# Four blocks by halves in front of a norm, three behind it, and split weights in the common tile ring

## The chip, the cores and the metric

The kernel runs on one core of a Trainium2 chip. The metric is device time in microseconds (us) of one execution; the median over several runs is compared. The engines are PE (TensorE, the matmuls), PEld (its weight loads), DVE (VectorE), ACT (ScalarE), POOL (GpSimd) and SP (SyncE, which issues most DMA transfers). Each engine works through its own list of instructions in the order that the program fixed, and waits where an operand is not ready or a buffer not free.

## The reference

512 tokens of 1024 features, float32. The part that matters here is the last step of the first block, and the shape of the two layers behind it.

```python
def rms_norm(x, g):
    y = x * lax.rsqrt(jnp.mean(x * x, axis=-1, keepdims=True) + EPS)
    return y * g
# block 1: forgetting attention, S5 scan, memory attention, gated and merged:
#   x = rms_norm(x + merged @ w_out, g_final)
# block 2, for l in 0, 1 (mod, gates: columns of silu(c) @ w_ada[l] + b_ada[l]):
#   h = rms_norm(x, g) * scale + shift;  x += gate * (dilated attentions(h) @ w_out[l])
#   h = rms_norm(x, g) * scale + shift;  x += gate * (relu(h @ w_f1)**2 @ w_f2)
```

(The second half of the code is told in shortened form.) A norm needs the sum of squares over all 1024 features of a token, so over all eight blocks of 128 features that the product in front of it makes, and every product behind it needs the normed tokens.

## The kernel before

**Products.** Activations lie feature-major: a tile holds 128 features of 512 tokens. Each float32 operand is split in two parts, hi and lo, and a product is three matmuls (hi by hi, lo by hi, hi by lo; `mm3`, L108 to L110). A block of 128 output features is 8 x 3 = 24 matmuls of 512 columns.

**Weights.** They come from HBM in 346 pieces of [128, 1024] (some are 768 wide) by SP's queue, into `wr` (3 buffers). `split` makes hi on ACT (`wh`, a cast, L88) and lo on DVE or POOL in turn (`wl`, a subtraction, L90). `wh` and `wl` have pools of their own, three buffers of [128, 1024] each. `get` splits three pieces ahead and fetches three more ahead of these.

**The ring.** Every other tile of 128 x 512 words (activations, logits, temporaries) comes from one ring of NU = 73 tiles. A tile is taken when the oldest with its place in the ring is released.

**In front of a norm.** `tail` makes the last two blocks of the product by halves of the tokens: first tokens 0 to 255 of both blocks, then tokens 256 to 511 of both. `post` adds the residual (DVE, `x`, L961 or L1070), squares it (ACT, `sq`, L174) and adds the squares up (DVE, `sacc`, L175). `tail` is called in eleven places: behind block 1 ("out"), behind the attention of each layer (`out0`, `out1`), and behind each of the four parts c of the MLP's second product (`f2`) in both layers.

**Behind a norm.** `norm` gives three stages for a half of the tokens. `stat`: sums over partitions (PE, `sumcols`, L181), mean (DVE, `nv`, L199), power -1/2 (POOL, `nr`, L201), broadcast (PE, `bcast`, L188). `hi`: x times scale times the broadcast (DVE, `hu`, L551) and `h` (ACT, L215), for eight blocks. `lo`: `l` (DVE, L223). `head` calls `stat(0)`, `hi(0)`, gets the weights, calls `stat(1)` and `lo(0)`, and then makes the first HN = 2 blocks of the next product by halves of the tokens, all products with `h` first (L584, L585) and those with `l` behind (L588). The norm between block 1 and layer 0 has a longer `stat` (L1067 to L1073, L1743 to L1746): two sums, a reciprocal, two powers on POOL and a product.

**The four norms that are followed by a head.** Here they are named by the product behind them: qa0 (block 1 to layer 0), f10 (MLP of layer 0), qa1 (layer 0 to layer 1), f11 (MLP of layer 1).

**Background.** `ada_gen` makes the modulation columns of a layer on DVE (`adacc`, L505, L511; `fin`, L482, on PE) beside other work; `drain` runs what is left of it. `load2` issues the rope and mask loads on ACT's queue.

**Order.** A scheduler lays down each engine's list when the program is built; the code's calls give the order in which work is offered to it.

Of the kernel before, what the change touches and what calls it, by code (L numbers as in the profile page):

```python
# [17 lines left out]
T = 512  # L18
# [9 lines left out]
class Core:  # L28
# [14 lines left out]
    NU = 73  # L43
    NW = 3, 3, 3

    def u(self, dt=F32, name="u"):
        """a [128, 512] tile of four-byte words from the common ring."""
        self.n += 1
        return self.ring.tile([128, T], dt, tag="u", name=f"{name}_{self.n}", bufs=self.NU)

# [28 lines left out]
    def split(self, i):  # L79
# [6 lines left out]
        h = self.t(self.wp, [128, 1024], F32R, "wh", self.NW[1])  # L86
        l = self.t(self.wp, [128, 1024], F32R, "wl", self.NW[2])
        self.nc.scalar.copy(h[:, 0:n], r[:, 0:n])  # L88
        eng = self.nc.gpsimd if i % self.WP == self.WP - 1 else self.nc.vector
        eng.tensor_tensor(out=l[:, 0:n], in0=r[:, 0:n], in1=f32(h)[:, 0:n], op=ALU.subtract)  # L90
        self.hl[i] = (h, l)

    def get(self, name, kb):
        """the next piece: hi and lo as [128, kb, columns]."""
# [7 lines left out]
        n = self.strips[i][1].shape[-1]  # L102
        return tuple(t[:, 0:n].rearrange("p (k c) -> p k c", k=kb) for t in self.hl.pop(i))

# [7 lines left out]
    def fm(self, out, w, c0, act, kb):  # L112
        """feature-major block: out[128 features, tokens] from strip columns c0..c0+128."""
        (wh, wl), (ah, al) = w, act
        for k in range(kb):
            self.mm3(out, wh[:, k, c0:c0 + 128], wl[:, k, c0:c0 + 128], ah[k], al[k], k == 0, k == kb - 1)

    def tm(self, out, ws, act, tok, cols=slice(0, 256)):
        """token-major block: out[128 tokens, cols]; ws: pieces that follow one another along k."""
        ah, al = act  # L120
        mm = self.nc.tensor.matmul
        ks = [(wh[:, k, cols], wl[:, k, cols]) for wh, wl in ws for k in range(wh.shape[1])]
# [31 lines left out]
    @staticmethod  # L154
    def half(t, hf):
        """half of the tokens: of four blocks of 128 in order, two."""
# [20 lines left out]
    def sumcols(self, pq, sacc, cols):  # L177
        """pq[:, i]: sums over features of the tokens of 128-blocks; cols: lists of first columns that add up."""
# [4 lines left out]
    def bcast(self, r):  # L183
        """columns r [128, n] -> [128, n * 128] in PSUM, the same in every row."""
# [7 lines left out]
    def rstd(self, sacc, cols):  # L192
        """broadcast of 1/sqrt(mean + eps), in PSUM."""
# [10 lines left out]
    def hsplit(self, src, bias=None, out=None):  # L204
        """hi, lo of src (+ bias)."""
# [20 lines left out]
class Att(Core):  # L226
    """Softmax attention on split operands. A head's logits come twice: query-major for the row
    maximum, key-major for the weights that multiply V and a block of ones, which sums them."""

    @staticmethod  # L230
    def cut(t, c):
        """columns c of t: a slice, or (i0, i1) for those of the tokens 4 i + r in the order (r, i)."""
# [5 lines left out]
    def byblock(t):  # L238
        """t, tokens 4 i + r in blocks of 128 and within these in the order (r, i), as [p, r, block, i]."""
# [24 lines left out]
    def turn(self, mc, psum_tag):  # L264
        """columns [128 tokens, 4, 128] -> rows [128, 512] in PSUM (exact)."""
# [5 lines left out]
    def rows(self, mc, tag, psum_tag, out=None):  # L271
        """the same as bf16 in SBUF; of these the last 32 if out is given."""
# [9 lines left out]
    def unit(self, nh, sregs, tregs, qk, vsl, dst, extra=None, nq=4, hd=64, orow=None, fold=None):  # L282
        """Items of a unit of nh heads (pairs of heads share 128 rows of output).
        sregs(qb): tiles of regions (c0, n, piece, q slice, k slice, mask)
        tregs(): tiles of (regions, [(v piece, kb, columns)])
        fold(j): the tile whose other half takes the rows of -max (else these come by a product of their own)
        qk(j, piece) -> pairs (q, k); vsl(j, piece, kb) -> (hi, lo); dst(j) -> (tile AP rows, row0)"""
# [118 lines left out]
        def vrow(j):  # L406
            """rows of a head's values in its sum; the other half holds the sum of the weights."""
# [41 lines left out]
    def mix(a, b, z=1.0):  # L449
        """a and b as one list, spread evenly, b over the first part z."""  # L450
# [3 lines left out]
    def merge(self, a, b):  # L454
        """run items of a with those of b spread evenly among them."""
# [13 lines left out]
class Blk2(Att):  # L469
    def ada_gen(self, l):  # L470
        """columns [128, 48] of silu(c) @ w_ada[l] + b_ada[l]."""
# [6 lines left out]
        def fin(acc, c):  # L478
            """acc: rows of two parts, c and c + 1"""
# [36 lines left out]
    def load2(self):  # L516
        """constants of the second block"""
# [21 lines left out]
    def norm(self, x, gcols, shcols, h):  # L539
        """by half of the tokens: hi and lo of rms(x) * g + shift. Returns the stages stat, hi, lo."""  # L540
# [21 lines left out]
    def plain(self, x):  # L562
        return lambda h, mod, ada: self.norm(x, mod[:, 0:8], ada[:, 0:8], h)
# [126 lines left out]
    HN = 2  # L690
# [1341 lines left out]
```

## Time and profile before

| | |
|---|---|
| median of 3 runs | 2513.65 us (2512.61 to 2514.68) |
| profiled execution, span | 2516.8 us |
| PE busy | 2388.2 us (95%), 12162 matmul instructions |
| DVE, ACT, POOL busy | 1533.0 (61%), 1038.1 (41%), 812.3 us (32%) |
| mean granted TensorE clock | 0.969 of full |

The profiled execution's only time on record is its span; it is 3.1 us over the median of the runs. PE is the busiest engine, and is idle in 129 us; what it loses besides lies in stretches at a lower granted clock, which the 40 slices of the page show as 8 or 7 where a full slice shows 9.

### The profile page before, as it was taken

What the parts mean: (1) busy time and instruction counts of PE and PEld (TensorE: products, weight loads), DVE (VectorE), ACT (ScalarE), POOL (GpSimd) and SP (SyncE); (2) the same over time, 40 slices, a digit from 0 to 9 for tenths busy, and PEclk for the clock granted to TensorE, in tenths of its full rate; (3) what the DMA queues carried; (4) which work ended last, traced back from release to release, by engine and by line L of the source; (5) the groups of instructions that cost most, each with busy time, mean ns of one, the idle gap of its engine ahead of it and who ended that gap; (6) DMA issues with size and microseconds to landing.
All of it is one profiled execution on the core that took longest, in us unless ns stands there. A gap on an engine that the chain in (4) does not pass through costs nothing. (4 is left out here: it accounts for less than half of the span.)

```text
span 2516.8 us, 32068 instructions
## 1 busy us (share of the span) xinstructions
PE 2388.2 (95%) x12162; PEld 1978.9 (79%) x12162; DVE 1533.0 (61%) x2394; ACT 1038.1 (41%) x1639; POOL 812.3 (32%) x601
## 2 busy tenths in 40 slices
PE   7999989989998889999999999998999999999999
PEld 6876778767888777787787888886777777888888
DVE  7667766666998887555459663258864726522222
ACT  4445543452333447533333423433663423423432
POOL 2445354634221552142122121227311612222121
PEclk9999999999998999998899999999999979999999
DMA  5311113213674321121138553233111313222232
GB/s 183 98 47 55 57 61 108 94 59 135 237 264 172 113 76 51 51 85 66 50 102 301 176 209 101 93 114 99 59 51 50 93 34 117 84 94 99 93 101 84
DMA packets 105610, 265.28 MB, mean 105 GB/s; under 512 B 13664, under 2 KB 23408, under 8 KB 105456
## 3 DMA queue, kind: packets, MB, share of 16 engines
q1 hardware_dynamic: 104304, 261.47, 31.2%
q8 instruction: 96, 1.57, 0.3%
q10 hardware_dynamic: 1152, 1.77, 0.2%
q14 instruction: 58, 0.48, 0.1%
HBM read 244.69 MB, written 9.44 MB: 101 GB/s over the span
## 5 line engine op out<-in xcount | busy, mean ns | idle before, releaser
L108 PE MATMUL pmm<-h,wh 128*128 128x512 f32 (+1 forms) x2232 | 855.7, 385 | 14.7 <-ACT h L213 3.9
L110 PE MATMUL pmm<-h,wl 128*128 128x512 f32 (+1 forms) x2232 | 852.9, 382 | 3.7 <-POOL wl L90 2.8
L109 PE MATMUL pmm<-l,wh 128*128 128x512 f32 (+1 forms) x2232 | 853.4, 383 | 0.0
L90 POOL TENSOR_TENSOR wl<-wr,wh 128x1024 fp32r<-128x1024 f32 (+1 forms) x173 | 422.5, 2442 | 1315.4 <-ACT wh L88 1094.4
L88 ACT CAST wh<-wr 128x1024 fp32r<-128x1024 f32 (+1 forms) x346 | 358.2, 1036 | 928.5 <-PE pmm L109 726.4
L108 PEld LDWEIGHTS pmm<-h,wh 128*128 128x128 f32 x2232 | 424.5, 190 | 96.7 <-ACT h L213 4.8
L110 PEld LDWEIGHTS pmm<-h,wl 128*128 128x128 f32 x2232 | 424.5, 190 | 82.5 <-POOL wl L90 3.8
L109 PEld LDWEIGHTS pmm<-l,wh 128*128 128x128 f32 x2232 | 425.2, 191 | 76.5 <-DVE l L221 0.7
L90 DVE TENSOR_TENSOR wl<-wr,wh 128x1024 fp32r<-128x1024 f32 (+1 forms) x173 | 225.1, 1301 | 168.9 <-ACT wh L88 166.5
L383 DVE TENSOR_TENSOR pl<-pe,ph 128x512 fp32r<-128x512 f32 (+4 forms) x168 | 121.7, 733 | 139.7 <-ACT ph L381 138.9
L961 DVE SCALAR_TENSOR_TENSOR x<-pmm,ada,x 128x512 f32<-128x512 f32 (+1 forms) x100 | 64.2, 643 | 213.9 <-PE pmm L110 213.7
L311 PE MATMUL ps<-qk,qk 128*128 128x512 f32 (+4 forms) x416 | 147.9, 386 | 16.1 <-POOL qk L672 9.6
L505 DVE SCALAR_TENSOR_TENSOR adacc<-adw,cact,adacc 128x512 f32<-128x512 f32 x168 | 154.3, 928 | 3.2 <-DMA adw<-in_wada 0.3
L221 DVE TENSOR_TENSOR l<-r,h 128x512 fp32r<-128x512 f32 x64 | 59.3, 928 | 121.6 <-ACT h L213 121.3
L379 ACT ACTIVATE pe<-ps 128x512 f32<-128x512 f32 (+4 forms) x168 | 84.5, 503 | 80.8 <-PE ps L311 72.7
L311 PEld LDWEIGHTS ps<-qk,qk 128*128 128x128 f32 x416 | 83.1, 204 | 37.7 <-POOL qk L672 11.5
L108 PE MATMUL pmm<-yh,wh 128*128 128x512 f32 (+1 forms) x244 | 94.1, 389 | 3.9 <-ACT yh L1403 2.4
L110 PE MATMUL pmm<-yh,wl 128*128 128x512 f32 (+1 forms) x244 | 93.7, 386 | 0.0
L109 PE MATMUL pmm<-yl,wh 128*128 128x512 f32 (+1 forms) x244 | 93.0, 382 | 0.0
L381 ACT CAST ph<-pe 128x512 fp32r<-128x512 f32 (+4 forms) x168 | 88.8, 528 | 9.4 <-DVE pl L383 3.5
L402 PE MATMUL ppv<-pl,v 128*128 128x512 f32 (+2 forms) x216 | 79.0, 366 | 4.1 <-DVE pl L383 4.0
L400 PE MATMUL ppv<-ph,v 128*128 128x512 f32 (+2 forms) x216 | 79.0, 366 | 2.7 <-ACT ph L381 1.6
(365 smaller groups left out, 3863.2 us busy)
## 6 DMA issues: line engine op xcount, KB each, us to landing
wr<-in_w SPq DMA_DIRECT2D x324, 512.0 KB
adw<-in_wada SPq DMA_DIRECT2D x192, 256.0 KB
xs<-xg SPq DMA_DIRECT2D x136, 64.0 KB
wr<-in_w SPq DMA_DIRECT2D x22, 384.0 KB
xd<-x SPq DMA_DIRECT2D x16, 256.0 KB
x<-xd SPq DMA_DIRECT2D x16, 256.0 KB
x<-in_x SPq DMA_DIRECT2D x16, 128.0 KB
x<-in_x SPq DMA_DIRECT2D x8, 256.0 KB
```

What stands on the lines that cost most here:

```text
L88: self.nc.scalar.copy(h[:, 0:n], r[:, 0:n])
L90: eng.tensor_tensor(out=l[:, 0:n], in0=r[:, 0:n], in1=f32(h)[:, 0:n], op=ALU.subtract)
L108: mm(out, wh, ah, start=start, stop=False)
L109: mm(out, wh, al, start=False, stop=False)
L110: mm(out, wl, ah, start=False, stop=stop)
L311: mm(outs[i] if len(r.shape) == 2 else outs[i].rearrange("p (r i) -> p r i", r=r.shape[1]), w, r, start=first and i == 0, stop=last and i ...
L379: nc.scalar.activation(out=e[:, w], in_=pt[:, w], func=AF.Exp)
L381: nc.scalar.copy(ph[:, w], e[:, w])
L383: nc.vector.tensor_tensor(out=pl[:, w], in0=e[:, w], in1=f32(ph)[:, w], op=ALU.subtract)
L400: mm(self.cut(pv, c), vh, h, start=f, stop=False)
L402: mm(self.cut(pv, c), vh, lo, start=False, stop=z)
L505: nc.vector.scalar_tensor_tensor(out=acc, in0=w, scalar=cc, in1=acc, op0=ALU.mult, op1=ALU.add)
```

## The change

The weight parts lose their own pools. A piece is split in two halves of 512 columns, each a tile `wh` and a tile `wl` of the ring, which grows from 73 to 85 tiles. `tail` now makes the last NT = 4 blocks by halves of the tokens in front of the four norms, and takes the fourth PSUM bank from those of the sums ("s"). The seven other tails change so: none for the MLP's parts c = 0, 1, 2 in either layer, two blocks as before at the very end. During its second half, `tail` issues `stat(0)` of the norm behind it after the first block, and `hi(0)` after the second; `head` then leaves both out (`begun`). `head` makes HN = 3 blocks by halves. The tiles of `h`, the modulation columns and the rest of the background are taken in front of the tail, and `load2` comes behind it. The number of matmuls is the same before and after, and so is the number of blocks by halves (22 in tails and 8 in heads before; 18 and 12 now).

```diff
-    NU = 73
-    NW = 3, 3, 3
+    NU = 85
+    NW = 3, 3
...
-        h = self.t(self.wp, [128, 1024], F32R, "wh", self.NW[1])
-        l = self.t(self.wp, [128, 1024], F32R, "wl", self.NW[2])
-        self.nc.scalar.copy(h[:, 0:n], r[:, 0:n])
         eng = self.nc.gpsimd if i % self.WP == self.WP - 1 else self.nc.vector
-        eng.tensor_tensor(out=l[:, 0:n], in0=r[:, 0:n], in1=f32(h)[:, 0:n], op=ALU.subtract)
-        self.hl[i] = (h, l)
+        self.hl[i] = []
+        for c in range(0, n, T):
+            m = min(T, n - c)
+            h, l = self.u(F32R, "wh"), self.u(F32R, "wl")
+            self.nc.scalar.copy(h[:, 0:m], r[:, c:c + m])
+            eng.tensor_tensor(out=l[:, 0:m], in0=r[:, c:c + m], in1=f32(h)[:, 0:m], op=ALU.subtract)
+            self.hl[i].append((h, l))
...
-    def head(self, names, h, posts, norm, view, byw=False):
+    def head(self, names, h, posts, norm, view, byw=False, begun=False):
         pms = [self.p("mm" if i else "pv") for i in range(len(names))]
         stat, hi, lo = norm
-        stat(0)
-        hi(0)
+        if not begun:
+            stat(0)
+            hi(0)
...
-    def tail(self, name, act, posts):
+    def tail(self, name, act, posts, norm=None):
         ws = [self.get(name, 8) for _ in posts]
-        pms = [self.p("mm") for _ in posts]
+        pms = [self.p("mm" if i < 3 else "s") for i in range(len(posts))]
         for hf in range(2):
             a = [[self.half(t, hf) for t in ts] for ts in act]
-            for w, pm, post in zip(ws, pms, posts):
+            for i, (w, pm, post) in enumerate(zip(ws, pms, posts)):
                 self.fm(self.half(pm, hf), w, 0, a, 8)
                 post(pm, slice(256 * hf, 256 * hf + 256))
                 self.tick(2.6)
+                if norm is not None and hf == 1 and i < 2:
+                    norm[i](0)
...
-    HN = 2
+    HN = 3
+    NT = 4
...
-        for s in range(3):
-            for f in self.strip(f"out{l}", xm, 8, [res(2 * s + b, 16, True) for b in range(2)]):
-                f()
-        self.tail(f"out{l}", xm, [res(6 + b, 16, True) for b in range(2)])
+        nt = self.NT
+        for f in self.strip(f"out{l}", xm, 8, [res(j, 16, True) for j in range(8 - nt)]):
+            f()
         h = self.new_h()
         norm = self.norm(x, mod[:, 8:16], ada[:, 24:32], h)
+        self.tail(f"out{l}", xm, [res(j, 16, True) for j in range(8 - nt, 8)], norm)
...
-                self.head([f"f1{l}"] * n, h, [relu2] * n, norm, self.half)
+                self.head([f"f1{l}"] * n, h, [relu2] * n, norm, self.half, begun=True)
             for f in self.strip(f"f1{l}", h, 8, [relu2] * (8 - n)):
                 f()
             sq = False if c < 3 else (None if out is not None else True)
-            for s in range(3):
-                for f in self.strip(f"f2{l}", F, 8, [res(2 * s + b, 40, sq) for b in range(2)]):
-                    f()
-            self.tail(f"f2{l}", F, [res(6 + b, 40, sq) for b in range(2)])
-        if l == 0:
-            self.drain(g)
-        return x
+            nt = 0 if c < 3 else 2 if out is not None else self.NT
+            for f in self.strip(f"f2{l}", F, 8, [res(j, 40, sq) for j in range(8 - nt)]):
+                f()
+            if c == 3:
+                norm = None
+                if out is None:
+                    del h
+                    self.drain(g)
+                    h = self.new_h()
+                    self.mod[l + 1] = self.mod_cols(l + 1)
+                    norm = self.norm(x, self.mod[l + 1][:, 0:8], self.ada[l + 1][:, 0:8], h)
+                self.tail(f"f2{l}", F, [res(j, 40, sq) for j in range(8 - nt, 8)], norm)
+        return x, h, norm
...
-        for s in range(3):
-            for f in self.strip("out", ms, 8, [res(2 * s), res(2 * s + 1)]):
-                f()
-        self.tail("out", ms, [res(6), res(7)])
+        nt = self.NT
+        for f in self.strip("out", ms, 8, [res(j) for j in range(8 - nt)]):
+            f()
+        while self.bg:
+            self.drain(self.bg[0])
...
+        h = self.new_h()
+        self.mod[0] = self.mod_cols(0)
+        norm = norm(h, self.mod[0], self.ada[0])
+        self.tail("out", ms, [res(j) for j in range(8 - nt, 8)], norm)
+        return xo, h, norm
...
-        x, norm = self.block1()
-        while self.bg:
-            self.drain(self.bg[0])
+        self.mod = {}
+        x, h, norm = self.block1()
         self.load2()
-        x = self.layer(0, norm, self.halfp, x)
-        self.layer(1, self.plain(x), self.half, x, out)
+        x, h, norm = self.layer(0, h, norm, self.halfp, x)
+        self.layer(1, h, norm, self.half, x, out)
```

Two places in the programs show how instructions move. PE at f10, before: `pmm_11631` is the last block by halves, L181 and L188 are sum and broadcast of the first half of the tokens, and L584 is the head.

```order
L109 MATMUL pmm_11631<-xl_11390,wh_11583 128x256
L110 MATMUL pmm_11631<-xh_11389,wl_11584 128x256
L181 MATMUL ps_11762<-c_2_67,sacc_11441 128x1 x2
L188 MATMUL ps_11769<-c_2_67,nr_11767 128x128 x2
L181 MATMUL ps_11808<-c_2_67,sacc_11441 128x1 x2
L584 MATMUL ppv_11760<-h_11744,wh_11618 128x256
L585 MATMUL ppv_11760<-h_11744,wl_11619 128x256
```

PE at f10, of the change: the lines are L113 to L115 for `mm3`, L186 for the sum, L193 for the broadcast, L587 and L588 for the head. `pmm_12339` and `pmm_12340` are the second and third of four blocks in the second half of the tokens, `ps_12341` the fourth; `h_12282` is the head's first operand.

```order
L113 MATMUL pmm_12339<-xh_12045,wh_12243 128x256
L186 MATMUL ps_12482<-c_2_67,sacc_12163 128x1 x2
L114 MATMUL pmm_12339<-xl_12046,wh_12243 128x256
...
L114 MATMUL pmm_12340<-xl_12069,wh_12302 128x256
L193 MATMUL ps_12489<-c_2_67,nr_12487 128x128 x2
L115 MATMUL pmm_12340<-xh_12068,wl_12303 128x256
...
L115 MATMUL ps_12341<-xh_12107,wl_12313 128x256
L587 MATMUL ppv_12600<-h_12282,wh_12318 128x256
L588 MATMUL ppv_12600<-h_12282,wl_12319 128x256
```

The sum has moved into the tail, with 28 matmuls of 256 columns between it and the broadcast, and 34 between the broadcast and the head; before, sum, broadcast and head stood next to one another. The second half's sum and broadcast (ahead of `l` in the head) now have 15 such matmuls between them.

ACT in layer 0's attention, before: `wh` are casts of weights, `qk` casts of a pair's queries and keys behind a product on DVE, `qr` and `vt` moves out of PSUM.

```order
L820 COPY vt_7994<-pmm_7932 128x512
L88 CAST wh_8139<-wr_7852 128x1024
L277 CAST qr_8014<-ps_8009 128x512
L650 CAST qk_7999<-xg_7774 64x512
L650 CAST qk_8004<-xg_7774 64x512
L758 CAST v_8028<-ps_8023 128x2x2x64
L758 CAST v_8030<-ps_8023 128x2x2x64
L277 CAST qr_8058<-ps_8053 128x512
L650 CAST qk_8043<-xg_7839 64x512
L88 CAST wh_8202<-wr_7930 128x1024
L650 CAST qk_8048<-xg_7839 64x512
```

The same place of the change:

```order
L825 COPY vt_8552<-pmm_8490 128x512
L282 CAST qr_8533<-ps_8528 128x512
L282 CAST qr_8572<-ps_8567 128x512
L656 CAST qk_8557<-xg_8312 64x512
L656 CAST qk_8562<-xg_8312 64x512
L765 CAST v_8586<-ps_8581 128x2x2x64
L765 CAST v_8588<-ps_8581 128x2x2x64
L282 CAST qr_8616<-ps_8611 128x512
L656 CAST qk_8601<-xg_8389 64x512
L656 CAST qk_8606<-xg_8389 64x512
L656 CAST qk_8621<-xg_8471 64x512
L656 CAST qk_8632<-xg_8471 64x512
```

Behind these stand `wh_8643` and `wh_8647`, the casts of the piece that PE uses next: they have moved from between the attention's casts to behind the last of them.

## Rows read from the trace of the kernel before

**Rows 1.** The page's span and its first engine (busy us, share, instructions).

```profile
span 2516.8 us, 32068 instructions
PE 2388.2 (95%) x12162; PEld 1978.9 (79%) x12162; DVE 1533.0 (61%) x2394; ACT 1038.1 (41%) x1639; POOL 812.3 (32%) x601
```

**Rows 2.** Timeline, f10: start, duration, engine, line, operation, tiles, idle before, releaser.

```profile
1295.56 0.50 PE L181 MATMUL ps<-c,sacc 128*128 128x1 f32 x4
...
1298.80 1.22 PE L188 MATMUL ps<-c,nr 128*128 128x128 f32 x4 [2.74 <-POOL nr L201]
...
1300.58 3.35 ACT L215 ACTIVATE h<-hu,ada 128x256 fp32r<-128x256 f32 x8 [3.14 <-DVE hu L551]
...
1301.14 0.58 PE L584 MATMUL ppv<-h,wh 128*128 128x256 f32 x1 [0.47 <-ACT h L215]
...
1303.02 1.05 PE L188 MATMUL ps<-c,nr 128*128 128x128 f32 x4
...
1305.58 0.33 PE L584 MATMUL ppv<-h,wh 128*128 128x256 f32 x1
```

**Rows 3.** Timeline of PE, qa1 (1666 us) and f11 (2152 us).

```profile
1666.29 0.28 PE L110 MATMUL pmm<-h,wl 128*128 128x256 f32 x1
1666.41 0.50 PE L181 MATMUL ps<-c,sacc 128*128 128x1 f32 x4
...
1674.38 0.28 PE L585 MATMUL ppv<-h,wl 128*128 128x256 f32 x1
...
2152.39 0.50 PE L181 MATMUL ps<-c,sacc 128*128 128x1 f32 x4
...
2162.41 0.29 PE L584 MATMUL ppv<-h,wh 128*128 128x256 f32 x1
```

**Rows 4.** Windows: stretch, length, busy of PE to POOL, granted clock, DMA.

```profile
785.00:790.00 5.00, 2.40 (x20) 2.20 (x19) 4.93 (x8) 2.18 (x3) 0.00 (x0) 1.00 0.22 85
790.00:800.00 10.00, 9.84 (x57) 9.87 (x58) 5.67 (x14) 2.88 (x6) 0.00 (x0) 0.66 0.16 52
1300.00:1305.00 5.00, 4.53 (x23) 4.44 (x22) 4.94 (x14) 3.35 (x8) 0.69 (x1) 0.50 0.24 88
```

**Rows 5.** Timeline of PE, qa0.

```profile
790.16 1.11 PE L482 MATMUL ps<-c,adacc 128*128 128x2 f32 x5 [2.76 <-DVE adacc L511]
...
803.28 0.95 PE L181 MATMUL ps<-c,sacc 128*128 128x1 f32 x8
...
808.65 1.19 PE L188 MATMUL ps<-c,nr 128*128 128x128 f32 x4 [4.42 <-DVE nr L1070]
...
814.14 0.29 PE L585 MATMUL ppv<-h,wl 128*128 128x256 f32 x1
```

**Rows 6.** Waits of PE: line, engine and line waited for, total us, times, longest.

```profile
PE ps L311 <- POOL qk L672: 9.6, 5, 2.2
...
PE pmm L110 <- POOL wl L90: 2.8, 4, 1.1
```

**Rows 7.** Timeline of PE behind the head of f10.

```profile
1329.15 0.50 PE L108 MATMUL pmm<-h,wh 128*128 128x512 f32 x1 [1.45 <-ACT r L984]
```

**Rows 8.** The page's groups of the splits (xcount, busy, mean ns, idle before).

```profile
L90 POOL TENSOR_TENSOR wl<-wr,wh 128x1024 fp32r<-128x1024 f32 (+1 forms) x173 | 422.5, 2442 | 1315.4 <-ACT wh L88 1094.4
L88 ACT CAST wh<-wr 128x1024 fp32r<-128x1024 f32 (+1 forms) x346 | 358.2, 1036 | 928.5 <-PE pmm L109 726.4
```

**Rows 9.** Lines by form: POOL on 512 columns (ns min, median, max).

```profile
L623 POOL TENSOR_TENSOR xg<-xg,rope x34: 1268/1396/1819, 842.6 to 1986.8; 128x512 f32<-128x512 f32 x34
```

**Rows 10.** Timeline of ACT, operations of 512 columns next to one another.

```profile
763.38 0.62 ACT L170 ACTIVATE sacc<-x 128x512 f32<-128x512 f32 x1
763.90 0.71 ACT L170 ACTIVATE sacc<-x,cols 128x512 f32<-128x512 f32 x1
```

**Rows 11.** Timeline of DVE and ACT, the end of a pair's queries and keys.

```profile
1979.37 0.68 DVE L635 TENSOR_TENSOR xg<-xg,ps 128x512 f32<-128x512 f32 x1
...
1980.08 1.26 ACT L650 CAST qk<-xg 64x512 fp32r<-64x512 f32 x2 [2.65 <-DVE xg L635]
```

More of the change, by code (lines that the diff above doesn't have):

```diff
@@ L101, in get @@
         self.iw += 1
-        n = self.strips[i][1].shape[-1]
-        return tuple(t[:, 0:n].rearrange("p (k c) -> p k c", k=kb) for t in self.hl.pop(i))
+        c = self.strips[i][1].shape[-1] // kb
+        per = T // c
+        hl = self.hl.pop(i)
+        self.hl[i] = None
+        return [tuple(t[:, c * (k % per):c * (k % per) + c] for t in hl[k // per]) for k in range(kb)]
     def mm3(self, out, wh, wl, ah, al, start=True, stop=True):
@@ L112, in fm @@
     def fm(self, out, w, c0, act, kb):
-        (wh, wl), (ah, al) = w, act
-        for k in range(kb):
-            self.mm3(out, wh[:, k, c0:c0 + 128], wl[:, k, c0:c0 + 128], ah[k], al[k], k == 0, k == kb - 1)
+        ah, al = act
+        for k, (wh, wl) in enumerate(w):
+            self.mm3(out, wh[:, c0:c0 + 128], wl[:, c0:c0 + 128], ah[k], al[k], k == 0, k == kb - 1)
     def tm(self, out, ws, act, tok, cols=slice(0, 256)):
@@ L121, in tm @@
         mm = self.nc.tensor.matmul
-        ks = [(wh[:, k, cols], wl[:, k, cols]) for wh, wl in ws for k in range(wh.shape[1])]
+        ks = [(wh[:, cols], wl[:, cols]) for w in ws for wh, wl in w]
         for k, (wh, wl) in enumerate(ks):
@@ L560, in norm @@
         return stat, hi, lo
-    def plain(self, x):
-        return lambda h, mod, ada: self.norm(x, mod[:, 0:8], ada[:, 0:8], h)
-    def head(self, names, h, posts, norm, view, byw=False):
+    def head(self, names, h, posts, norm, view, byw=False, begun=False):
         pms = [self.p("mm" if i else "pv") for i in range(len(names))]
         stat, hi, lo = norm
-        stat(0)
-        hi(0)
+        if not begun:
+            stat(0)
+            hi(0)
         ws = [self.get(n, 8) for n in names]
@@ L582, in head @@
                 for k in range(8):
-                    for (wh, wl), o in g:
-                        mm(o, wh[:, k, :], ah[k], start=k == 0, stop=False)
-                        mm(o, wl[:, k, :], ah[k], start=False, stop=False)
+                    for w, o in g:
+                        mm(o, w[k][0], ah[k], start=k == 0, stop=False)
+                        mm(o, w[k][1], ah[k], start=False, stop=False)
                 for k in range(8):
-                    for (wh, wl), o in g:
-                        mm(o, wh[:, k, :], al[k], start=False, stop=k == 7)
+                    for w, o in g:
+                        mm(o, w[k][0], al[k], start=False, stop=k == 7)
         for pm, post in zip(pms, posts):
@@ L780, in tm_items, with layer @@
         return [lambda g=g: f(g) for g in range(4 // per)]
-    def layer(self, l, norm, view, x, out=None):
+    def layer(self, l, h, norm, view, x, out=None):
         nc = self.nc
-        ada = self.ada[l]
-        mod = self.mod_cols(l)
+        ada, mod = self.ada[l], self.mod[l]
         xd = self.xdram[l]
-        h = self.new_h()
         Y = {}
@@ L805, in layer @@
         ps = [post(cq, self.CA, self.SA, True, ("a", b)) for b in range(4)]
-        self.head([f"qa{l}"] * self.HN, h, ps[0:self.HN], norm(h, mod, ada), view)
+        self.head([f"qa{l}"] * self.HN, h, ps[0:self.HN], norm, view, begun=True)
         for j in range(8):
@@ L1767, in s5_out @@
         self.gfm = self.t(self.base, [128, 8], F32, "gfm")
-        return xo, norm
+        h = self.new_h()
[3 more added lines that the diff above has]
+        return xo, h, norm
 PERM = np.arange(T).reshape(128, 4).T.reshape(-1)
```

## The prediction

> **What bounds the kernel now.** I read the page first. PE is busy in 95% of the span, 2388.2 of 2516.8 us [rows 1]; the other engines are far from full, so what can be won is PE's idle time (129 us) and the stretches in which its clock is granted at half. The matmuls themselves neither come nor go. The list of PE's waits shows where the idle time ends, and the timeline and windows then show what the four norms cost, since a wait there is followed by a lower clock.
>
> At f10 the last product of the tail is done at 1295.56. Then PE does the sums, waits 2.74 us for POOL's power, broadcasts, waits for the first `h`, and begins the head at 1301.14; the first matmul at full rate starts at 1305.58 [rows 2]. [...] The reader is to see that the stall is paid twice: as idle time, and then as 16 matmuls of the head at half rate.
>
> What is lost there: from 1295.56 to 1305.58 are 10.0 us. Needed in it are 16 matmuls at 0.12, 1.9 us, two sums of 0.50, and two broadcasts at half of the 1.05 that one shows at half clock, together 2.0 [rows 2]. Lost: 6.1. f11 has the same interval, 2152.39 to 2162.41 [rows 3], so 6.1 again. qa1 runs from 1666.41 to 1674.38 [rows 3], 8.0 us with 9 matmuls of the head: 8.0 - 1.1 - 2.0 = 4.9. The three plain norms cost **17.1 us**.
>
> At qa0 there are two stalls. Before the second half of the tail PE waits 2.8 us for the end of the background (`adacc`), while DVE is busy in 4.93 of 5 us; behind it the clock is 0.66 over 10 us, which is 3.4 us lost [rows 4, 5]. Then the sum at 803.28, a wait of 4.4 us for the long `stat`, and full rate from 814.14 on: 10.9 us, of which 13 matmuls of the head (1.6), two sums of 0.95 and one broadcast at about 0.6 are needed; 6.8 lost [rows 5]. qa0 costs **13.0 us**.
>
> **The change, part by part.**
>
> *The sums and broadcasts inside the tail, plain norms.* From sum to broadcast takes 3.24 us at f10 (1295.56 to 1298.80) [rows 2]. PE's new order has 28 matmuls of 256 columns there, 28 x 0.12 = 3.4 us: just covered. From broadcast to head takes 2.34 us [rows 2]; 34 matmuls give 4.1. The second half is not covered: 15 matmuls, 1.8 us, stand between its sum and broadcast, and the same 3.2 us are wanted. What is late next is therefore the broadcast of the second half, by 1.3 us, with the products of `l` queued behind it on PE. Such a wait costs from 0 (the scheduler's list has the sum as early as it can be) to 3 (the sum's followers on DVE or POOL stand behind a split; a half split on POOL is 1.27, [rows 9]). I take 1.3 for each norm, 3.9 in all, and no half clock behind so short a wait; none in these rows shows what a wait of that length does to the clock, and a bound for it is 1.5 us more each, 16 matmuls by 0.09 as at f10. Gain: 17.1 - 3.9 = **13.2**.
>
> *Three head blocks instead of two.* The third piece's products stand between the first two pieces' `h` products and those with `l`, 32 matmuls behind the head's start. Its casts on ACT come behind all eight `h`, which take 3.35 us [rows 2]. Those now begin while the tail's last 34 matmuls run, so the weights have some 4.1 + 3.8 us from the broadcast, against 1.8 to the first `h`, 3.35, and two squares and a cast (0.5 to 0.6 each [rows 10], 1.6): 6.8. Covered, by 1 us. Cost 0; were the cover gone, up to 1 us each.
>
> *qa0.* The drain of the background now stands in front of the tail, and `fin` on PE comes 78 matmuls later than before, so the 2.8 and the 3.4 go: 6.2 gained (bound from below 3, if DVE, full in that stretch, now delays the residuals instead). The long `stat` does not fit: 9 matmuls (1.1 us) stand between sum and broadcast, where PE waited 4.4 us before [rows 5]. I expect 2 to 3.3 us of wait (less than 4.4 - 1.1 as far as DVE's other work in between has moved away), then 1.4 to `h`, then half clock: of the 6.8 lost, 5 stay. Gain 6.2 + 1.8 = **8.0**. The rope and mask issues, which now follow `hi(0)` on ACT's queue, delay the third piece of that head by some 2 us; I leave that inside the 5.
>
> *Halved blocks.* 30 blocks by halves before, 30 after: a halved block costs more than a whole one, but the number is unchanged. 0.
>
> *Weights behind the heads.* Behind the heads PE waits for POOL's subtractions (2.8 us in four waits) and once 1.45 us on other work in the same crowd [rows 6, 7]. With the subtraction in two halves the first is done in 1.27 instead of 2.4 [rows 8, 9], and three pieces instead of two are in place: **3** of these 4.2 go.
>
> *The splits in two.* 346 casts become 692. On ACT a cast of 1024 is 1.04 us [rows 8], and operations of 512 follow each other at 0.52, the last running 0.62 [rows 10]: two take 1.14, 0.10 more, 35 us on ACT, whose busy share is 41%. On POOL two of 1.27 against 2.44 [rows 8, 9], 0.1 more. Beside PE this is free, as long as no cast is awaited. [...]
>
> *The ring instead of pools.* The pools held six tiles of 1024 columns, which are twelve of the ring; 73 + 12 = 85, so no space is lost or won. But a split now takes its tiles in turn with everything else. The order of ACT in layer 0's attention shows what that does: the cast of the piece that PE needs next now stands behind the last `qk` of its pair, where before it stood between earlier ones. Its product is the next that PE has. I find some ten such places (three in each layer's attention, four in block 1). The price of one: DVE's product 0.68, two casts of `qk` 1.26, the weight's cast 0.6, 2.5 us [rows 11], less what PE has left to do meanwhile; from 0 (PE works through the logits that the same `qk` release) to 2.5. Most have one to four matmuls of 512 columns in hand. I take 0.8 each, **8 us lost** (0 to 16 for the range; 25 at the most).
>
> **Sum.** 13.2 + 8.0 + 3 - 8 = 16.2 us gained. 2516.8 - 16.2 = 2500.6 in a profile; the runs' median stands 3.1 under the profile's span, so **2497.5**.
>
> **Rivals.**
>
> *The gain is eaten by late weights.* If each of the ten places costs the full 2.5 us, they cost 25 and the sum is -0.8: about 2514. For it: PE already waits for such a `qk` elsewhere, 9.6 us in five waits [rows 6]. Against: one wait per place would have to find no work at all in front of it.
>
> *Slower: the ring runs short.* The mechanism is one place, the weight cast on ACT: where it waits for a tile of the ring that attention still holds, PE stops until a pair is done, and the next cast is late as well. Price 2.5 us each by the same rows. The other gains of 24.2 us and 5 more for a visible loss ask for twelve such waits, 30 us; with twelve to fifteen the time is 2519 to 2527, I name 2522. Against: the lookahead is three pieces as before, and the space is the same.
>
> *The clock falls all the same.* If the 1.3 us of the second broadcast, or the wait at qa0, are enough for half clock, each plain norm keeps some 4 of its losses and qa0 all 6.8: gain 17.1 - 12 + 6.2 + 3 - 8 = 6.3, 2507.4. For it: at f10 a wait of 2.74 was followed by half clock [rows 2, 4]; against: PE is full in the tail up to the wait.
>
> *The list is not the time.* If DVE is late with the residuals of four blocks, sum and broadcast stand in PE's list where their operands aren't there, and stop the tail that was to cover them; nothing is gained at the plain norms. That leaves 8.0 + 3 - 8 = 3 us: 2516.8 - 3 - 3.1 = about 2511, no change. For it: DVE is full ahead of qa0 [rows 4]; against: over the kernel it is busy in 61%.
>
> **How the numbers follow.** My forecast gets 0.52, late weights 0.14, the ring 0.12, the clock 0.14, DVE late 0.08. 0.2% of this kernel is 5 us, about what a measurement can tell from no change: faster means under 2508.6, slower over 2518.7. Forecast and clock lie under it mostly, with a part of the late weights: faster 0.70; same 0.18; slower 0.12. The range goes from 2484 (nothing lost in attention, half of the norms' 3.9 saved, more from qa0) to 2517.
>
> **What would show it.** Right: no half clock at f10, qa1 and f11; the broadcast's wait there gone; PE's wait on `adacc` gone; waits of PE for `wh` and `wl` of up to 8 us new in the attention stretches. Wrong: waits for ACT's `wh` over 20 us, or ACT idle before `wh` on releases of the ring; the head starting with 0.21 us spacing; DVE behind PE by more than a block inside a tail.

## Result, and the profile after

The changed kernel took 2499.71 us (median of 4 runs, 2499.02 to 2500.55), the kernel before 2513.43 in runs beside it: a ratio of 0.9945, 95% interval 0.9931 to 0.9959, 13.7 us faster. 2497.5 was forecast. In the experiments, on three chips, the kernel before ranged from 2495 to 2528 us, at a mean granted clock of 0.975 in the shortest runs and 0.961 in the longest, so the comparisons below go by ratios to runs of before on the same chip. (The ratios given are not the quotients of the two medians; the two differ by up to 0.2%.)

The page of the changed kernel: span, and busy time of each engine.

```profile
span 2497.4 us, 33134 instructions
PE 2367.7 (95%) x12162; PEld 1956.8 (78%) x12162; DVE 1532.0 (61%) x2573; ACT 1065.5 (43%) x1995; POOL 858.1 (34%) x774
```

Beside [rows 1] the span is 19.4 us shorter, and PE's busy time 20.5. The number of matmuls is the same and PE's idle time nearly so (129 and 130 us). What was won therefore lies in matmuls that ran at a higher clock, not in less waiting: added up over windows of 5 us, the half clock lost 78.5 us before and 56.3 now. The waits changed places.

The two profiles differ by 19.4 us, the runs by 13.7. In the other traces a span stands 1.7 to 2.3 us below the time of its run (1.85 for the changed kernel). By that I estimate that the profiled execution of before, with its span of 2516.8, took some 2518.6 us, 5 more than the median of its runs. So the sums by profiles below hold about 5 us that belong to the two executions and not to the change.

**The norms.** Timeline of PE at f10 in the changed kernel, the places of [rows 2] (first half of the tokens, then the second):

```profile
1296.55 0.50 PE L186 MATMUL ps<-c,sacc 128*128 128x1 f32 x4
...
1300.35 0.60 PE L193 MATMUL ps<-c,nr 128*128 128x128 f32 x4
...
1304.86 0.28 PE L587 MATMUL ppv<-h,wh 128*128 128x256 f32 x1
...
1308.82 0.51 PE L186 MATMUL ps<-c,sacc 128*128 128x1 f32 x4
...
1311.78 0.71 PE L193 MATMUL ps<-c,nr 128*128 128x128 f32 x4 [0.56 <-POOL nr L206]
...
1313.30 0.39 PE L591 MATMUL ppv<-l,wh 128*128 128x256 f32 x1 [0.81 <-DVE l L228]
...
1317.00 0.39 PE L587 MATMUL ppv<-h,wh 128*128 128x256 f32 x1 [0.31 <-ACT h L220]
```

In the first half, sum, broadcast and head stand in the stream without a wait, 3.8 us from sum to broadcast, and the head's matmuls follow at 0.12 us from the first one on (the next starts at 1304.98): no half clock. Three short waits are left in the second half.

**qa0.** The same view:

```profile
792.10 0.39 PE L113 MATMUL pmm<-yh,wh 128*128 128x256 f32 x1 [1.39 <-ACT wh L91]
796.75 0.39 PE L115 MATMUL pmm<-yh,wl 128*128 128x256 f32 x1 [0.92 <-DVE wl L92]
803.44 1.02 PE L487 MATMUL ps<-c,adacc 128*128 128x2 f32 x8 [0.18 <-DVE adacc L516]
...
814.42 0.68 PE L193 MATMUL ps<-c,nr 128*128 128x128 f32 x4 [1.06 <-DVE nr L1081]
816.45 0.58 PE L587 MATMUL ppv<-h,wh 128*128 128x256 f32 x1 [1.34 <-ACT h L220]
...
819.18 0.41 PE L587 MATMUL ppv<-h,wh 128*128 128x256 f32 x1
819.39 0.38 PE L588 MATMUL ppv<-h,wl 128*128 128x256 f32 x1
819.60 0.29 PE L587 MATMUL pmm<-h,wh 128*128 128x256 f32 x1
```

The wait for the background fell from 2.76 [rows 5] to 0.18. At the head the clock still falls: 0.21 us from matmul to matmul up to 819.60.

**Weight parts.** All of PE's waits for weight parts in the changed kernel (total us, times, longest):

```profile
PE pmm L115 <- POOL wl L92: 5.0, 5, 2.4
PE pmm L113 <- ACT wh L91: 4.7, 4, 1.9
PE pmm L130 <- POOL wl L92: 2.2, 3, 1.8
PE ppv L587 <- ACT wh L91: 1.6, 1, 1.6
PE pmm L129 <- ACT wh L91: 1.3, 2, 0.8
PE pmm L588 <- DVE wl L92: 1.2, 1, 1.2
PE pmm L130 <- DVE wl L92: 1.1, 2, 0.7
PE pmm L115 <- DVE wl L92: 0.9, 1, 0.9
```

18.0 us in 19 waits; the same rows of before add up to 4.4.

**A gain that the prediction did not have.** The attention of the second pair of heads in each layer (about 1190 and 2040 us). Windows of the kernel before, where the column behind POOL's busy time is the granted clock:

```profile
1184.00:1212.00 28.00, 28.00 (x102) 21.53 (x103) 5.47 (x11) 10.98 (x26) 0.00 (x0) 0.57 0.05 18
2036.00:2068.00 32.00, 32.00 (x107) 24.36 (x107) 5.47 (x11) 11.56 (x26) 0.00 (x0) 0.52 0.05 16
```

and of the changed kernel:

```profile
1188.00:1200.00 12.00, 12.00 (x43) 8.15 (x43) 2.88 (x5) 6.01 (x13) 2.53 (x2) 0.72 0.10 28
...
2028.00:2036.00 8.00, 8.00 (x27) 5.50 (x26) 2.04 (x3) 4.64 (x11) 2.52 (x2) 0.58 0.18 63
2036.00:2068.00 32.00, 32.00 (x179) 26.04 (x178) 6.33 (x12) 13.27 (x28) 4.01 (x4) 1.00 0.15 51
```

PE was busy all the time in all of these windows. Before, the clock lost 28 x 0.43 + 32 x 0.48 = 27.4 us there; now 12 x 0.28 + 8 x 0.42 = 6.7. That is 20.7 us, more than the whole gain. What PE did when the clock fell, in the kernel before:

```profile
2035.75 0.33 PE L311 MATMUL ps<-qk,qk 128*128 128x128 f32 x1
2036.01 0.39 PE L311 MATMUL ps<-qk,kl 64*128 64x128 f32 x1
2036.33 0.47 PE L311 MATMUL ps<-qk,qk 128*128 128x128 f32 x1
2036.73 0.47 PE L311 MATMUL ps<-qk,kl 64*128 64x128 f32 x1
```

Logits and sums of short matmuls, one behind another without a gap: in PE's list stand 104 of them there with no matmul of a weight between. In the changed kernel's list the longest such run in this attention is 32. Nothing in the change's text speaks of this attention; the scheduler laid it down differently.

### The profile page after: what moved, and what is told of

Same layout as the page of the kernel before. It is cut to its first block, busy times and chain, and to the rows that moved or that the text cites. A ratio compares the mean times of both kernels' runs of the same rounds, so it can differ in the third digit from the quotient of the medians.

```text
span 2497.4 us, 33134 instructions
## 1 busy us (share of the span) xinstructions
PE 2367.7 (95%) x12162; PEld 1956.8 (78%) x12162; DVE 1532.0 (61%) x2573; ACT 1065.5 (43%) x1995; POOL 858.1 (34%) x774
## 4 chain that ended last, share of the span: by engine, by line
PE 66%; DVE 11%; issue 3%; ACT 3%; POOL 2%; DMA 1%; SPq 0%; DVEq 0%; POOLq 0%; ACTq 0%
PE pmm L113 17%; PE pmm L115 17%; PE pmm L114 17%; PE ps L316 5%; DVE wl L92 1%; DVE adacc L510 1%; PE ppv L406 1%; PE ppv L405 1%; PE ppv L407 1%; DVE unm L341 1%; DVE l L228 1%; DVE qk L662 1%; PE pmm L130 1%; PE pmm L131 1%; DVE xs L630 1%
## 5 line engine op out<-in xcount | busy, mean ns | idle before, releaser
L92 POOL TENSOR_TENSOR wl<-wr,wh 128x512 fp32r<-128x512 f32 x346 | 480.9, 1409 | 1176.4 <-ACT wh L91 994.7
L113 PE MATMUL pmm<-h,wh 128*128 128x512 f32 (+1 forms) x2104 | 822.7, 392 | 5.4 <-ACT wh L91 2.8
L115 PE MATMUL pmm<-h,wl 128*128 128x512 f32 (+1 forms) x2104 | 818.7, 390 | 4.5 <-POOL wl L92 4.3
L114 PE MATMUL pmm<-l,wh 128*128 128x512 f32 (+1 forms) x2104 | 818.2, 389 | 0.0
L115 PEld LDWEIGHTS pmm<-h,wl 128*128 128x128 f32 x2104 | 398.3, 189 | 87.7 <-POOL wl L92 6.4
L113 PEld LDWEIGHTS pmm<-h,wh 128*128 128x128 f32 x2104 | 399.1, 190 | 83.7 <-ACT wh L91 4.0
L114 PEld LDWEIGHTS pmm<-l,wh 128*128 128x128 f32 x2104 | 398.9, 190 | 77.6 <-issue 0.4
L91 ACT CAST wh<-wr 128x512 fp32r<-128x512 f32 (+1 forms) x692 | 385.2, 610 | 134.2 <-DMA wr<-in_w 101.9
L92 DVE TENSOR_TENSOR wl<-wr,wh 128x512 fp32r<-128x512 f32 x346 | 285.4, 853 | 58.3 <-ACT wh L91 48.8
L989 ACT ACTIVATE r<-pmm 128x512 f32<-128x512 f32 x62 | 37.0, 597 | 273.0 <-PE pmm L115 273.0
L113 PE MATMUL pmm<-yh,wh 128*128 128x512 f32 (+1 forms) x244 | 91.5, 378 | 6.0 <-ACT yh L1414 4.0
L626 POOL TENSOR_TENSOR qv<-qv,mhalf 128x8 f32<-128x8 f32 x34 | 61.8, 1819 | 89.8 <-DVE qv L625 86.3
L115 PE MATMUL pmm<-yh,wl 128*128 128x512 f32 (+1 forms) x244 | 90.9, 374 | 1.7 <-DVE wl L92 0.9
```

Of the source, the lines that this page charges most:

```text
L91: self.nc.scalar.copy(h[:, 0:m], r[:, c:c + m])
L92: eng.tensor_tensor(out=l[:, 0:m], in0=r[:, c:c + m], in1=f32(h)[:, 0:m], op=ALU.subtract)
L113: mm(out, wh, ah, start=start, stop=False)
L114: mm(out, wh, al, start=False, stop=False)
L115: mm(out, wl, ah, start=False, stop=stop)
L626: nc.gpsimd.tensor_tensor(out=v, in0=v, in1=self.mhalf, op=ALU.pow)
```

## Experiments

Where the time lies is best seen by stages. Start of the first head matmul to the next, in the profiles (us; the first column ends at block 1's head, the others at qa0, f10, qa1, f11 and the start of the last matmul; each row is one execution):

| kernel | start | block 1 | attention 0 | MLP 0 | attention 1 | MLP 1 |
|---|---|---|---|---|---|---|
| before | 16.6 | 794.6 | 489.9 | 370.3 | 486.5 | 355.3 |
| changed | 20.2 | 796.2 | 488.4 | 360.6 | 475.3 | 353.2 |
| changed, again | 19.4 | 793.3 | 488.8 | 360.6 | 475.0 | 353.3 |
| ring alone | 20.1 | 799.8 | 486.3 | 368.7 | 479.4 | 356.6 |
| tails alone | 16.0 | 787.0 | 495.2 | 371.8 | 502.2 | 359.2 |
| before, NG = 8 | 16.6 | 797.2 | 480.2 | 369.3 | 477.6 | 355.0 |
| before, NG = 0 | 16.6 | 802.1 | 496.6 | 370.3 | 489.0 | 355.6 |
| split four ahead | 19.9 | 818.3 | 488.4 | 361.5 | 476.0 | 354.3 |

**The ring alone.** The kernel before with this edit, which brings the splits in two with it, and the products indexed to suit:

```diff
-    NU = 73
-    NW = 3, 3, 3
+    NU = 85
+    NW = 3, 3
...
+        for c in range(0, n, T):
+            m = min(T, n - c)
+            h, l = self.u(F32R, "wh"), self.u(F32R, "wl")
```

> The kernel before with the weight parts in the ring of 85 tiles and nothing else of the change. Theory A (a third of the gain comes from the new order of the attention, not from the norms): the two stretches of half clock in the attention of the second pair, 12.0 and 15.4 us in the profile of before, shrink to under 5 each, 20 us won; PE waits for weight parts some 18 us instead of 4.4 and the rest of block 1 loses a few us; the four norms cost what they did. About 2508 us (2500 to 2516). Theory B (the prediction's sum: norms and nothing else won, late weights lost): the late weights alone, 8 us more than before, about 2521 us.

Measured: 2517.39 us, 1.0003 of before (0.9989 to 1.0017): no change. The stretches of half clock shrank as theory A had it, to 36 x 0.14 + 32 x 0.11 = 8.6 us:

```profile
1184.00:1220.00 36.00, 36.00 (x172) 27.43 (x171) 6.56 (x11) 14.26 (x29) 5.03 (x4) 0.86 0.13 45
2036.00:2068.00 32.00, 32.00 (x160) 24.65 (x160) 6.29 (x11) 14.27 (x29) 5.06 (x4) 0.89 0.15 50
```

and PE's waits for weight parts rose to 13.8 us. The two attention stages won 10.7 us, the start and block 1 lost 8.7, 6.3 of them to more half clock in block 1. So the ring, with its splits in two, brings the new order of the attention, and by itself it is worth nothing in sum. Theory A's mechanism held; its 2508 was too low by what the start and block 1 lost.

**Tails and heads alone.** The changed kernel with the weight parts in pools of three pieces:

```diff
-    NU = 85
-    NW = 3, 3
+    NU = 73
+    NW = 3, 3, 3
...
+        h = self.t(self.wp, [128, 1024], F32R, "wh", self.NW[1])
+        l = self.t(self.wp, [128, 1024], F32R, "wl", self.NW[2])
```

> The change with the weight parts left in their own pools of three pieces and a ring of 73. Theory A: four pieces cannot be held by three buffers, and the scheduler's list has the fourth block's first half behind most of the second half, and sum and broadcast next to one another behind the tail; the plain norms win nothing, qa0 wins its wait for the background and the half clock behind it, some 6 us; the long stretches of half clock in the second pair's attention stay (12 and 15 us). About 2507 us (2502 to 2514). Theory B: what the tails win needs no ring, 24 us, about 2489 us.

Measured: 2533.45 us, 1.0063 (1.0039 to 1.0087): slower, where one theory had 2507 and the other 2489. PE at f10 in that kernel (L183 the sum, L190 the broadcast, L584 the head):

```profile
1294.84 0.50 PE L183 MATMUL ps<-c,sacc 128*128 128x1 f32 x4
1296.42 0.71 PE L190 MATMUL ps<-c,nr 128*128 128x128 f32 x4 [1.08 <-POOL nr L203]
1298.25 0.39 PE L584 MATMUL ppv<-h,wh 128*128 128x256 f32 x1 [1.12 <-ACT h L217]
```

As theory A had it, sum, broadcast and head stand next to one another (for the second half too, with waits of 1.03 and 1.11), since a fourth piece finds no buffer. The long stretches of half clock stayed (clock 0.52 and 0.57 over 32 us each). The loss came in places that neither theory named: 15.7 us in attention 1, 5.3 in attention 0. In attention 1 the half clock lost 35.8 us instead of 28.2, and PE was idle for 32.4 instead of 26.0; what brings that about was not tried. Neither part of the change, as built here, is worth anything alone; the two together are. Tails with pools of their own for four pieces were not run.

**The clock in the second pair's attention.** NG is the number of gate blocks that are offered among its logits. Three kernels change that number alone (8 or 0 for 5):

```diff
-    NG = 5
+    NG = 8
```

> The kernel before with NG = 8 instead of 5: all eight gate blocks are offered among the logits of the second pair's attention, and the longest run of matmuls without one of a weight in PE's list is 50 instead of 104. Theory A (the long stretch of half clock belongs to that run of short matmuls): the stretches of 12 and 15 us shrink to under 6 each, 10 to 18 us won: 2496 to 2504 us. Theory B (the clock there is no matter of the order): 2513 us, within 3.

> The kernel before with NG = 0: no gate block is offered in the second half of the second pair's attention, and the longest run without a weight's matmul there is 144 instead of 104. Theory A (half clock belongs to the run): the two stretches of half clock grow from 12 and 15 us to 15 to 20 each, 5 to 10 us slower than before, 2520 to 2526 us. Theory B: as before, 2513 to 2516 us.

> The changed kernel with NG = 0 instead of 5: no gate block is offered among the second half of the second pair's attention; the longest run without a weight's matmul there is 66 again. Theory A: the half clock in the two stretches grows from 3.4 us to 8 to 15 each, 10 to 20 us lost: 2508 to 2520 us. Theory B: 2500 us, within 3.

Measured: before with NG = 8 2505.63 us, 0.9971 (0.9946 to 0.9995); before with NG = 0 2528.96, 1.0038 (1.0006 to 1.0070); the changed kernel with NG = 0 2504.38, 0.9964 (0.9943 to 0.9985), which can't be told from the changed kernel by the intervals and is less than the 10 to 20 us that theory A asked for. Windows of before with NG = 8, and then with NG = 0:

```profile
1176.00:1212.00 36.00, 36.00 (x197) 28.40 (x196) 8.16 (x16) 15.53 (x30) 4.76 (x2) 1.00 0.13 44
2028.00:2060.00 32.00, 32.00 (x163) 25.78 (x162) 6.21 (x10) 12.84 (x27) 2.37 (x1) 0.89 0.10 33
```

```profile
1192.00:1228.00 36.00, 36.00 (x136) 29.03 (x136) 7.65 (x13) 13.04 (x30) 0.00 (x0) 0.53 0.03 12
2056.00:2088.00 32.00, 32.00 (x125) 25.91 (x124) 5.06 (x11) 11.76 (x27) 0.00 (x0) 0.52 0.01 3
```

One number, and no work added or left out, takes the loss from 27.4 us to 32 x 0.11 = 3.5 or to 32.3. The longest run without a weight's matmul in PE's list there, and the loss of the clock in the two stretches by such windows:

| kernel | longest run | lost, us |
|---|---|---|
| before, NG = 0 | 144 | 32.3 |
| before | 104 | 27.4 |
| tails alone | 104 | 29.1 |
| split four ahead | 73 | 18.9 |
| changed, NG = 0 | 66 | 13.6 |
| split four ahead, NG = 8 | 60 | 11.8 |
| before, NG = 8 | 50 | 3.5 |
| ring alone; changed | 32 | 8.6; 6.7 |

The loss goes with the run, but for the last two rows. It comes back from execution to execution: in the five other traces with a longest run of 32 (the changed kernel again, NT = 2, NT = 3, HN = 2 and the ring of 87) the two stretches lost 6.8 to 8.5 us. In the attention stages of the profiles NG = 8 won 18.6 us, in the runs 7.3 (0.0029 x 2513). Most of the difference lies in the executions that were profiled: that of NG = 8 took 2501.45 us, 4.2 under its median, and that of before some 5 over its own.

**The changed kernel again, and its numbers of blocks.**

> The changed kernel itself, beside the kernel before on one chip with the runs below. The kernel before ranged from 2497 to 2526 us here, with the mean granted clock. Theory A (norms, the clock in the attention, and late weights against them): 0.9945 of before within 0.002, some 2499 us, the clock of its profile 0.975 or more. Theory B (the gain first measured was a draw of the clock): within 0.2% of before.

Measured: 2500.50 us, 0.9957 (0.9938 to 0.9977), clock 0.977.

```diff
-    NT = 4
+    NT = 2
```

> The changed kernel with two blocks by halves in front of a norm. PE's list then has 15 matmuls of 256 columns between sum and broadcast instead of 28, and none between broadcast and head instead of 34. Theory A (it is the cover of four blocks that wins at the norms): f10, qa1 and f11 each wait 1.4 us for the broadcast and 2.3 for the first h, and lose half clock behind it, 4 us more each than in the changed kernel: 12 us, about 2511 us, no more than before. Theory B (the stages issued early win by themselves): 2500 us, within 4.

Measured: 2507.92 us, 0.9985 (0.9963 to 1.0008), no longer to be told from before. Waits of the size that theory A named are there, but on other operands: at f10 PE waits 1.13 us for `sacc` with the sum of the second half and 2.31 for `l`:

```profile
1309.07 0.58 PE L186 MATMUL ps<-c,sacc 128*128 128x1 f32 x4 [1.13 <-DVE sacc L180]
...
1318.36 0.39 PE L591 MATMUL ppv<-l,wh 128*128 128x256 f32 x1 [2.31 <-DVE l L228]
```

> The changed kernel with three blocks by halves in front of a norm: PE's list has 28 matmuls between sum and broadcast, as with four, but 9 between broadcast and head, 1.1 us of the 2.3 that the first h takes. Theory A (cover counts): a wait of about 1.2 us at each plain norm, 4 us in all, about 2503 to 2505 us, between the 2500.5 of four blocks and the 2507.9 of two. Theory B: no difference from four, 2500 within 2.

Measured: 2507.42 us in company of a slower 2517.93 of before, 0.9953 (0.9938 to 0.9968): as four blocks, within the intervals. By the runs theory B, or a difference under 4 us.

> The changed kernel with two head blocks instead of three. PE's list has 5 matmuls between the second half's sum and its broadcast instead of 15, with the products of l around them. Theory A: the second broadcast comes about 1 us later at each norm and PE waits for weight parts behind the heads again, 1 us each; 4 to 8 us slower than the changed kernel, 2504 to 2508 us. Theory B: the third block does nothing, within 3 us of the changed kernel.

Measured: 2503.34 us, 0.9965 (0.9942 to 0.9987). 2 us from the changed kernel by the ratios, inside the intervals of both: the runs alone leave open whether the third head block does anything.

The traces show more than these times. PE's waits and the half clock at the three plain norms together (f10, qa1, f11; one execution each, us):

| kernel | waits | lost to half clock |
|---|---|---|
| before | 9.9 | 8.5 |
| NT = 2, HN = 3 | 10.1 | 5.1 |
| NT = 3, HN = 3 | 9.0 | 3.4 |
| NT = 4, HN = 2 | 6.2 | 5.1 |
| changed (NT = 4, HN = 3) | 5.0 | 0.0 |

Each block that is left out brings waits and half clock back. Without the third head block PE waits 1.7 us for `l` at each of the three norms, and half clock follows at all three; the changed kernel's waits of 0.81 and less are followed by none. By this reading the third head block is worth some 6 us at these norms, and the fourth tail block some 7; the runs show neither. (NT = 3 and HN = 2 have 96 matmuls fewer than the changed kernel and NT = 2 has 192 fewer, since more blocks are made whole. In the kernel before, matmuls of 512 columns stand 0.227 us apart at full clock, from 1399.83 to 1403.91, and those of 256 0.12, so I estimate 5.4 us for a block made whole, 24 x 0.227, and 5.8 for one by halves, 48 x 0.12.)

**More room for the weights.**

> The changed kernel with the weights split four pieces ahead instead of three, in the same ring of 85 tiles. Theory A (the 18 us of waits for weight parts come from casts that stand late in ACT's list): more than half of them go, 10 us won, about 2490 us. Theory B (the ring is short): the waits of the attention for its own tiles grow by as much or more, 2500 us or slower.

The edit is `NW = 3, 4`. Measured: 2518.48 us, 1.0024 (1.0001 to 1.0047). The waits for weight parts fell to 6.5 us, as theory A said, and the time rose all the same. I first took the half clock that came back in the second pair's attention (18.9 us) for the cause:

> The kernel that splits four pieces ahead, with NG = 8: the longest run without a weight's matmul in the second pair's attention is 60 instead of 73. In that kernel's profile PE waited 6.5 us for weight parts (18.0 in the changed kernel), but the half clock in that attention was back at 10.2 and 8.5 us, and the time was 2518. Theory A (the new order's half clock ate what the weights gave): the two stretches fall to under 5 each and the time by 8 to 12 us, about 2508. Theory B (the ring is short, and the waits of the attention itself make it slow): within 4 us of 2518.

Measured: 2520.27 us, 1.0014 (0.9994 to 1.0035): theory A fell, although the clock there lost 7 us less. The stages say why: attention and MLP took what they do in the changed kernel, and block 1 took 22 us more (818.3; 820.0 with NG = 8). In the profile with NG = 5 the half clock lost 37.5 us in block 1 instead of 22.3, and PE was idle there for 61 instead of 47, most of the increase on DVE's `s5b` and `gt` and on POOL's `qk`. That the ring's 85 tiles are short there is a guess; no run shows what holds these back.

> The changed kernel with two buffers of raw weights instead of three and the ring at 87 tiles. Theory A (the ring's size is not what limits): nothing won by two tiles; the raw weights come later and PE's waits for weight parts stay or grow; 2500 to 2506 us. Theory B (the ring is short): waits in the attention fall, 2495 us or less.

The edit is `NU = 87`, `NW = 2, 3`. Measured: 2520.70 us, 1.0001 (0.9985 to 1.0016), 0.4% over the changed kernel: all stages from attention 0 on grew by 4 to 6 us. Two more tiles don't pay for one buffer of raw weights less.

No version here beats the changed kernel.

## Why the prediction was right, and where it was not

The time and the sign were right, and the norms were right in mechanism. That the time came out 2.2 us from the forecast is luck: the largest gain was not in the sum at all, and the other terms together came out 17.5 us lower than foreseen. Without the half clock won in the second pair's attention the profiles would show no gain. By the profiles, us won (+) or lost (-):

| term | predicted | measured |
|---|---|---|
| three plain norms | +13.2 | +9.6 |
| qa0, without weights | +8.0 | +8.9 |
| waits for weight parts (behind heads +3, late -8) | -5 | -13.6 |
| half clock in the second pair's attention | 0 | +20.7 |
| the rest | 0 | -6.2 |
| sum | +16.2 | +19.4 |

The sum then took the median to stand 3.1 us under the span, as for the kernel before; the changed kernel's runs stand above it, so 2500.6 was forecast for a profile of 2497.4 and 2497.5 for runs of 2499.7.

**Plain norms.** The cover of 28 and 34 matmuls held: no wait, no half clock in the first half. The second broadcast was late, as said, by 0.56; what the step mis-sized is what comes behind it: `l` 0.81 late and the next `h` 0.31. With the restart after each wait and the products of `l` (0.13 apart for 0.12) a norm loses 2.5 us, not 1.3, so 17.1 - 7.5 = 9.6. f11 and qa1 show the same rows. NT = 2 takes most of the cover away, and waits and half clock come back. The 0.12 us in the sums of what is lost is the spacing of matmuls of 256 columns ahead of the wait at qa1, from 1666.29 on in [rows 3], at a granted clock of 1.00 from 1660 to 1665; the half rate of the 16 matmuls at f10 is the 0.50 of [rows 4].

**qa0.** The background's wait went, with its half clock, 6 us as predicted. The rival that the clock falls all the same came true here alone. Left are 1.1 and 1.3 of waits, some 1.4 of half clock, and in the second half 0.2, 1.2 and 0.5, 5.9 with what it takes to resume; before it was 13.0, another 1.6 on `l` and 0.2 on `h`, so 8.9 won. Two further waits for weight parts (1.39 and 0.92) lie in the tail, which wants four pieces at once, and one (1.23) in the head. The six rope and mask issues on ACT's queue, some 2 us by the prediction, ran from 818.88 to 821.69, 2.8 us, and the next cast began at 821.79.

**Behind the heads** the waits for POOL's splits at f10 and f11 are gone, as said.

**Late weights: the step that failed.** I read ten places out of ACT's list, most of them in the attention of the layers, and put 0.8 us on each. The waits are there, but elsewhere: in both layers only three are left (0.7, 0.5 and 0.7 us); the rest lie at the start, in block 1 and in qa0's tail and head, the longest two here:

```profile
521.82 0.50 PE L113 MATMUL pmm<-h,wh 128*128 128x512 f32 x1 [1.92 <-ACT wh L91]
...
536.98 0.50 PE L115 MATMUL pmm<-h,wl 128*128 128x512 f32 x1 [2.39 <-POOL wl L92]
```

At the places that I named PE waits for the queries and keys themselves, and the cast behind them is done by the time these are used. In layer 0 it is so (ACT, then PE):

```profile
892.83 1.14 ACT L91 CAST wh<-wr 128x512 fp32r<-128x512 f32 x2
```

```profile
894.37 2.07 PE L316 MATMUL ps<-qk,qk 128*128 128x512 f32 x4 [3.70 <-POOL qk L678]
896.24 0.63 PE L113 MATMUL pmm<-h,wh 128*128 128x512 f32 x1
```

That a cast stands directly behind an operation that PE awaits does not make it the last to come.

**The order of the attention.** I read the list for what stands in front of a weight's cast and not for what PE's stream looks like. The row of the page that counts PE's clock in 40 slices had its lowest figure, 7, at 2013 to 2076 us, and 8 on both sides of 1195: the two stretches stood in the profile of before and were larger than what all plain norms lost. I read the clock only where I expected it to fall.

**The splits in two.** ACT's busy time rose by 27.4 us (35 estimated from rows). A cast of 512 lasts 0.61 us on the mean in the profile, but the next starts before it ends, and two take 1.14 (above, at 892.83). POOL's splits rose from 2.44 to 2 x 1.39 us, 0.34 more where I had 0.1.

**The rest**, 6.2 lost, is half clock in places that the table does not name. At the start and in block 1 it lost 22.2 us in the changed kernel instead of 17.1, 3.4 of them behind this wait, which the kernel before does not have:

```profile
34.37 0.58 PE L591 MATMUL ppv<-l,wh 128*128 128x256 f32 x1 [5.95 <-DVE l L226]
```

In the layers' attention outside the second pair's stretches it lost 25.6 instead of 18.9; five of its eight stretches there stand at waits of 3.4 to 6.1 us, four of these for DVE's `mcq`. PE's other waits fell by some 3 us. So the new order won 20.7 us of clock in one place and lost 11.8 in others. No run here undoes these alone.

## What to carry to other kernels

A change that moves buffers can move the scheduler's whole order; compare the new list of the busiest engine with the old one over the whole program, not only where the change was meant to act, and ask of each stretch what clock it had. Add up the lost clock over the whole trace as well: more than half of what this change won in one attention it lost elsewhere. Work that covers a chain has to be counted in the new list from each link to the next, as far as the last consumer: the half that was covered gave what was predicted, the half behind it twice the predicted loss. Two parts that are each worth nothing (the ring) or less than nothing (the tails) can be worth something together, so test them alone before you judge either.

## What the runs showed of the hardware

TensorE's clock fell to half while PE was busy without a gap, in runs of short matmuls of the attention (0.50 from 1188 to 1208 and from 2040 to 2064 in the kernel before), and stayed there for 24 and 31 us (34 with NG = 0). In the kernel before, matmuls of the weights came back into the stream at 1208.28 and 2062.19, first 0.43 to 0.57 us apart, and 0.23 from 1210.12 and 2066.95 on. How it falls behind a wait was known from [rows 2, 4]; this was not.

Some small operations on DVE lasted as long as POOL's large ones beside them, 1.17 to 1.20 us against 1.26. DVE in the changed kernel, and then POOL in the same stretch:

```profile
856.74 1.19 DVE L263 CAST mcq<-qv 128x8 bf16<-128x8 f32 x1
857.97 1.17 DVE L264 TENSOR_TENSOR sp<-qv,mcq 128x8 f32<-128x8 f32 x1
...
860.41 1.18 DVE L266 TENSOR_TENSOR sp<-sp,mcq 128x8 f32<-128x8 f32 x1
...
861.62 0.18 DVE L267 CAST mcq<-sp 128x8 bf16<-128x8 f32 x1
```

```profile
856.64 1.26 POOL L92 TENSOR_TENSOR wl<-wr,wh 128x512 fp32r<-128x512 f32 x1
857.86 1.26 POOL L629 TENSOR_TENSOR xg<-xg,rope 128x512 f32<-128x512 f32 x1
859.08 1.26 POOL L92 TENSOR_TENSOR wl<-wr,wh 128x512 fp32r<-128x512 f32 x1
```

The operations on 128 x 8 take 1.2 us each, in step with POOL's, and the next, with POOL idle, 0.18. PE waits 5.5 us for the end of this chain, at 861.85. In the changed kernel 36 of the 224 operations on 128 x 8 in such chains (`qv`, `sp`, `mcq`) last over 1 us, in the kernel before 25, and each of these stands beside an operation of POOL. No run shows what brings that about.
